# Key/value units between gate/up units, and deeper tiles for the attention's probabilities, in a decoder trunk on one core

## The chip, the core and the metric

One Trainium2 chip, one of its cores. The metric is device time in microseconds (us) of one execution. The engines are named as in the profile: PE (TensorE, matmuls), PEld (its weight loads), DVE (VectorE), ACT (ScalarE), POOL (GpSimd) and SP (SyncE, which here only issues transfers). Work tiles live in SBUF; matmuls write to PSUM, which the kernel uses in tiles of 128 x 512 fp32 (called banks below).

## What is computed

Two layers over 256 tokens of width 1024 in fp32. Each layer is half a feed-forward, a mixer, and half a feed-forward again, each behind an RMS norm and added to h:

```python
def _swiglu(x, w_gate_up, w_down):
    a, b = jnp.split(x @ w_gate_up, 2, axis=-1)      # 2 x 2816 columns
    return (jax.nn.silu(a) * b) @ w_down

for layer in range(DEPTH):
    h = h + 0.5 * _swiglu(_rmsnorm(h, ...), ...)
    hn = _rmsnorm(h, mix_norm[layer])
    if layer < N_A_LAYERS: h = h + _short_conv(hn, ...)
    else:                  h = h + _nsa(hn, ..., *shared)
    h = h + 0.5 * _swiglu(_rmsnorm(h, ...), ...)
    if layer == N_A_LAYERS - 1:
        shared = _shared_kv(h, ...)
```

So there are four feed-forwards. `_shared_kv` makes, from the h behind the second of them, the keys and values that the attention `_nsa` of the second layer uses: two slots are compressed (blocks of 32 tokens through a two-layer network), two slots of keys are normed, two slots of values are kept. Its result is needed only by the attention, that is behind the third feed-forward, which starts from the same h.

## The kernel before

**Arithmetic.** Each fp32 weight is split into two parts, `whi` (ACT casts it to the PE's fp32r format) and `wlo` (DVE subtracts: raw - whi); activations are split likewise (`hg` for normed inputs, `gg` for gated products). A product of two split numbers needs three matmuls, or a 512-column one and a 256-column one.

**Units.** The program is a list of units (`unit`, `run_units`). A unit with weights loads one `raw` tile of up to 128 x 2048 fp32 (1 MB; three buffers), splits it in two halves into `whi` and `wlo` (three buffers each), does its matmuls, and has a `post` that reads the result from PSUM. `run_units` loads three units ahead and splits two ahead.

- A *gate/up unit* (`gate_up(ft)`, 22 of them, here g0, g1, ...) does 16 pairs of matmuls into a pair of PSUM banks `pa`; its post sums the two halves and scales them on ACT and DVE (`t`), takes silu on ACT (`s`), and multiplies on POOL (`g<-s,t`). One unit later `g` is split into `gg`. 16 *down units* follow, which read `gg`.
- `shared_kv` has ten units: raw slots r0, r1 (48 matmuls of 256 columns; DVE then writes the tile `rt` out of `pa` in eight pieces, POOL adds positions to give two `rf`, ACT and DVE split them to `r`); token-major units t00, t01 (keys, both into one pair of banks) and t10, t11 (values); and compression units c00, c01, c10, c11, with only 16 matmuls of 256 columns each on 1 MB of weights. Small steps between them (`k_transposes`, `hidden`, `second_k`, `second_k2`, `second_v`) hang on a unit at a given step, by the table `KVSEQ`.

`pa` has two pairs of banks (`psA`, 2 buffers of 2 banks), used in turn by whatever unit comes next.

**Order.** The order is not the program's. A planner (`Plan.schedule`) takes every instruction with its dependencies and an estimated cost, and lays out a fixed order for each engine by list scheduling; each engine then works its own queue strictly in that order. Program order sets where two instructions stand if nothing else does, which buffer is reused after which, and which units can be split ahead of which.

**Stages.** Feed-forward 0 (from 0 us), convolution (from about 195 us), feed-forward 1 (from 295), the ten key/value units (470 to 521), feed-forward 2 (to 705), attention with its query and output projections (to 815), feed-forward 3. The calls, from the end of `program`:

```python
    u = shared_kv("n3", G_KV)
    norm_hooks("n3", u)
    ffn(2, "n3", G_FFN + 16, "n4", [G_MIX + 8], own_pool("g2"))
    u = nsa("n4", G_MIX + 8, "n5", [G_FFN + 24])
```

**Memory.** SBUF pools of the stages follow one another: `stage_pool` opens a pool `after` the one before, and the first writer of the new pool waits for all users of the old. The key/value units' tiles are in `kvp`, feed-forward 2's `gg` in `g2`, the attention's tiles in `nsap`.

**Attention.** For each of 24 steps PE computes scores (`S<-kth,qs`), DVE takes the maximum (`mx`), ACT the exponentials (`P`, five buffers), POOL weights them (`P<-P,pw`), PE transposes them (`pb<-cst,P`), ACT casts the transposes (`ph`), DVE subtracts (`pl`; `ph` and `pl` have `PB` = 2 buffers each), and PE multiplies with the values (`pc<-ph,vhl`). The output projection's first units run between these steps.

Of the kernel before, what the change touches and what calls it, by code (L numbers as in the profile page):

```python
# [134 lines left out]
class PlanPool:  # L135
    def __init__(self, plan, name, bufs, psum=False, after=None):
        self.plan, self.name, self.bufs, self.psum, self.after = plan, name, bufs, psum, after
        self.tags = {}
        self.tiles = []
        self.real = self.stack = None  # L140
# [70 lines left out]
class Plan:  # L211
# [8 lines left out]
    def pool(self, name, bufs, psum=False, after=None):  # L220
        p = PlanPool(self, name, bufs, psum, after)
        self.pools.append(p)
        return p
# [171 lines left out]
    def replay(self, tc, order, engines, stack):  # L395
        opened = {}

        def real_pool(p):
            if p.real is None:
                if p.after is not None and p.after.stack is not None:  # L400
                    p.after.stack.close()
                p.stack = ExitStack()
                kw = {"space": PSUM} if p.psum else {}
                p.real = p.stack.enter_context(tc.tile_pool(name=p.name, bufs=p.bufs, **kw))
            return p.real

        for p in self.pools:
            if p.after is None:
                real_pool(p)
# [22 lines left out]
def program(plan, a, out, ones):  # L432
# [9 lines left out]
    chain = {"sb": None, "ps": psA}  # L442

    def stage_pool(name):
        p = chain["sb"] = plan.pool(name, 1, after=chain["sb"])
        return p

    def wide_psum(name, bufs):
        wide["pool"] = chain["ps"] = plan.pool(name, bufs, psum=True, after=chain["ps"])
# [211 lines left out]
    def ffn(lf, nkey, gname, okey, ogains, pool_open):  # L661
# [6 lines left out]
        def gate_up(ft):  # L668
# [38 lines left out]
        def down(dt, c):  # L707
            def mm(wh, wl):
                if c == 0:
                    st["pd"] = psB.tile([128, 512], F32, name="pb")  # L710
                yield from halves_mm(st["pd"], (wh[:, :HALF * 128], wl[:, :HALF * 128]), c * HALF,
                                      st["gg"], c == 0, c == 1)
# [6 lines left out]
        u0 = gate_up(0)  # L719
        for ft in range(1, NF):  # L720
# [6 lines left out]
    def own_pool(name):  # L727
        def op(st):
            st["pool"] = stage_pool(name)
        return op  # L730

# [85 lines left out]
    def shared_kv(nkey, gname):  # L817
        st = {}

        def rawslot(s):  # L820
            def mm(wh, wl):
                if s == 0:
                    own_pool("kvp")(st)
                    st["kvc"] = st["pool"].tile([128, NKVC], F32, name="kvc")
                    sp.dma_start(st["kvc"], a["kvc"])
                    st["rt"] = [st["pool"].tile([128, 528], F32, name=f"rt{x}") for x in range(2)]
                    for x in range(2):
                        gp.memset(st["rt"][x][:, 512:], 0.0)
                    ac.copy(kcs, zero[:, :1].to_broadcast([128, 608]))
                    for q in range(2):  # L830
                        for ab in range(2):
                            xp = slice(64 - ab * 64, 128 - ab * 64)
                            o = kth[q][ab][xp].rearrange("p b j n -> p (b j n)")
                            ac.copy(o, zero[xp, :1].to_broadcast([64, 512]))
                st["ps"] = two_banks()
# [5 lines left out]
            def post():  # L841
                ps = st["ps"]
                R = NORM[nkey].R
                for j in range(2):
                    for gg in range(2):
                        hp = slice(gg * 64, gg * 64 + 64)
                        g = 2 * j + gg
                        for p in range(2):
                            tt(ve, st["rt"][s][p * 64:p * 64 + 64, g * 128:(g + 1) * 128],
                               ps[hp, j, p:T:2], R[hp, p:T:2], ALU.mult)  # L850
                for hh in range(2):
# [3 lines left out]
                       st["rt"][s].rearrange("p (a b) -> p a b", b=8),  # L855
# [176 lines left out]
        u0 = None  # L1032
        for name, *hooks in KVSEQ:
            u = make[name]() if name else u + 1
            u0 = u if u0 is None else u0
            for x, f in hooks:
                at_mid(u, x, side[f])
                late[u] = x
        return u0


    def nsa(nkey, gname, okey, ogains):
# [527 lines left out]
```

## Time and profile before

| | |
|---|---|
| median of three runs | 1002.56 us (999.06 to 1004.71) |
| the profiled execution's own time | 1002.02 us |
| its span | 1000.2 us |
| mean granted PE clock | 0.998 |
| PE busy | 985.0 us (98%), 5792 instructions |
| PEld busy | 859.4 us (86%) |
| DVE busy | 727.5 us (73%) |
| ACT busy | 585.7 us (59%) |
| POOL busy | 207.9 us (21%) |
| read from HBM | 175.80 MB, 177 GB/s over the span |

The profile is one execution, and lines of it give an engine, an operation, the tile it writes and those it reads (`wlo<-raw,whi`), all at line 419, since one helper issues everything; so one goes by tiles. The span runs from the first instruction to the last; the execution's own time is 1.8 us longer. Matmuls are pipelined and their ends are modelled, so PE's busy time holds short waits too. In the timeline a row is a run of like instructions, with its start, its length and, in brackets, how long the engine stood idle before it and what ended that.

### The profile page before, as it was taken

The page shows a single profiled execution, that of the slowest core. Times are in us where ns is not written, and L with a number is a line of the kernel's source. Part 1 is how long each engine was busy: PE and PEld are TensorE (multiplying, and loading weights), DVE is VectorE, ACT ScalarE, POOL GpSimd, SP SyncE. Part 2 cuts the span into 40 slices and gives each one's busy share as a digit, 9 for nine tenths or more (in the row PEclk, how much of TensorE's full clock was granted, in tenths as well). Part 3 has the DMA queues.
Part 4 walks back from the last instruction along what each step waited for, and adds up shares of the span by engine and source line. Part 5 has one row for each costly group of instructions (what it writes and reads, how often), then busy time and mean ns, then how long its engine had stood idle before and what let it go on. Part 6 is the DMA issues. An engine that isn't in the chain of part 4 may idle for free.

```text
span 1000.2 us, 15237 instructions
## 1 busy us (share of the span) xinstructions
PE 985.0 (98%) x5792; PEld 859.4 (86%) x5792; DVE 727.5 (73%) x1086; ACT 585.7 (59%) x1049; POOL 207.9 (21%) x266
## 2 busy tenths in 40 slices
PE   8999999999999999999999999999998999999998
PEld 6888888888888888889878888888897888888887
DVE  6876766688797676677889776666788787676554
ACT  8665554445465555555586656545599765555441
POOL 2211111021221111111331111100578531111100
PEclk9999999999999999999999999999999999999999
DMA  8655455655655555456366655365511245554353
GB/s 280 239 206 176 163 173 175 201 183 190 213 179 200 192 187 168 152 200 247 131 234 214 222 173 194 120 202 195 204 62 43 79 172 175 197 179 161 127 194 108
DMA packets 31033, 177.83 MB, mean 178 GB/s; under 512 B 3440, under 2 KB 6000, under 8 KB 16112
## 3 DMA queue, kind: packets, MB, share of 16 engines
q1 hardware_dynamic: 30960, 176.86, 51.4%
q8 instruction: 45, 0.74, 0.3%
q14 instruction: 28, 0.23, 0.1%
HBM read 175.80 MB, written 1.05 MB: 177 GB/s over the span
## 4 chain that ended last, share of the span: by engine, by line
PE 88%; DVE 4%; ACT 4%; issue 1%; POOL 1%; DMA 1%; SPq 0%; ACTq 0%; DVEq 0%; POOLq 0%
PE pa L419 52%; PE pb L419 29%; PE S L419 4%; PE pc L419 3%; DVE wlo L419 1%; ACT P L419 1%; ACT whi L419 1%; DVE hg L419 1%; DMA raw<-in_wgu_dram 1%; DVE px L419 0%; POOL rf L419 0%; DMA px<-in_px_dram 0%; ACT kth L419 0%; DVE s L419 0%; POOL hg L419 0%
## 5 line engine op out<-in xcount | busy, mean ns | idle before, releaser
L419 PE MATMUL pa<-hg,whi 128*128 128x512 f32 (+1 forms) x1568 | 538.8, 390 | 1.7 <-DVE hg L419 1.6
L419 DVE TENSOR_TENSOR wlo<-raw,whi 128x1024 fp32r<-128x1024 f32 (+4 forms) x383 | 412.1, 1093 | 163.8 <-ACT whi L419 162.3
L419 ACT CAST whi<-raw 128x1024 fp32r<-128x1024 f32 (+3 forms) x388 | 350.7, 927 | 198.8 <-issue 81.9
L419 PE MATMUL pa<-hg,wlo 128*128 128x256 f32 x1536 | 430.8, 281 | 0.4 <-DVE wlo L419 0.4
L419 PEld LDWEIGHTS pa<-hg,whi 128*128 128x128 f32 x1568 | 291.6, 187 | 67.8 <-DVE hg L419 3.6
L419 PEld LDWEIGHTS pa<-hg,wlo 128*128 128x128 f32 x1536 | 290.3, 189 | 1.3 <-DVE wlo L419 1.1
L419 PE MATMUL pb<-gg,whi 128*128 128x512 f32 x704 | 245.1, 394 | 0.0
L419 PE MATMUL pb<-gg,wlo 128*128 128x256 f32 x704 | 195.7, 279 | 0.0
L419 PEld LDWEIGHTS pb<-gg,whi 128*128 128x128 f32 x704 | 131.8, 187 | 30.3
L419 POOL TENSOR_TENSOR g<-s,t 128x256 f32<-128x256 f32 x88 | 71.0, 807 | 413.6 <-ACT s L419 409.7
L419 PEld LDWEIGHTS pb<-gg,wlo 128*128 128x128 f32 x704 | 132.7, 188 | 0.3
L419 ACT ACTIVATE s<-t 128x256 f32<-128x256 f32 x88 | 36.7, 417 | 137.5 <-DVE t L419 137.5
L419 POOL TENSOR_TENSOR acc<-acc,sq 128x256 f32<-128x256 f32 x36 | 33.6, 934 | 177.0 <-ACT sq L419 176.4
L419 DVE TENSOR_TENSOR t<-pa,t 128x512 f32<-128x512 f32 x94 | 64.3, 684 | 3.6 <-ACT t L419 3.5
L419 DVE TENSOR_TENSOR t<-t,R 128x512 f32<-128x512 f32 x96 | 65.7, 685 | 0.1
L419 ACT COPY t<-pa 128x512 f32<-128x512 f32 x94 | 54.2, 576 | 2.9 <-PE pa L419 2.8
L419 PE MATMUL S<-hg,whi 128*128 128x256 f32 (+1 forms) x224 | 48.7, 302 | 1.6 <-DVE hg L419 1.3
L419 DVE SCALAR_TENSOR_TENSOR px<-pb,px 128x256 f32<-128x256 f32 x56 | 23.7, 423 | 34.8 <-PE pb L419 33.9
L419 PE MATMUL pb<-hg,whi 128*128 128x512 f32 (+1 forms) x144 | 48.2, 386 | 0.0
L419 DVE TENSOR_TENSOR gg<-g,gg 128x256 fp32r<-128x256 f32 x88 | 36.8, 419 | 13.1 <-ACT gg L419 13.1
L419 ACT CAST gg<-g 128x256 fp32r<-128x256 f32 x88 | 35.4, 403 | 13.9 <-POOL g L419 12.6
L419 DVE SCALAR_TENSOR_TENSOR hg<-px,hg 128x256 fp32r<-128x256 f32 x56 | 40.1, 734 | 1.4 <-ACT hg L419 1.1
(176 smaller groups left out, 876.4 us busy)
## 6 DMA issues: line engine op xcount, KB each, us to landing
raw<-in_wgu_dram SPq DMA_DIRECT2D x86, 1024.0 KB, 4.8
raw<-in_wdn_dram SPq DMA_DIRECT2D x64, 704.0 KB, 4.2
raw<-in_wci_dram SPq DMA_DIRECT2D x8, 1024.0 KB, 5.1
raw<-in_wci_dram SPq DMA_DIRECT2D x8, 512.0 KB, 3.6
raw<-in_wco_dram SPq DMA_DIRECT2D x4, 1024.0 KB, 4.8
raw<-in_wkt_dram SPq DMA_DIRECT2D x4, 1024.0 KB, 4.8
raw<-in_wc_dram SPq DMA_DIRECT2D x4, 1024.0 KB, 4.8
raw<-in_wq_dram SPq DMA_DIRECT2D x4, 1024.0 KB, 4.8
```

The source lines that it names most:

```text
L419: getattr(engines[op.eng], op.name)(*[real(x) for x in op.args], **{k: real(v) for k, v in op.kw.items()})
```

## The change

It does five things.

1. The ten key/value units, which stood ahead of the third feed-forward, stand between its first eight gate/up units. `KVSEQ` (a list) becomes `KVAT` (which units come ahead of which gate/up unit), `shared_kv` returns a function `between(ft)`, and `ffn` calls it ahead of each `gate_up(ft)`. The order of weights is now r0 g0 r1 g1 t00 t01 g2 c00 g3 c01 g4 t10 t11 g5 c10 g6 c11 g7 g8 and so on.
2. `gg` becomes two tiles of eleven units each, in all four feed-forwards. In the third, the first half is in a pool `g20` on the right side of SBUF, which lives beside `kvp`; the second half's pool `g21` follows `kvp` (`beside_kv`). A pool may now follow several others.
3. The two `rt` tiles are allocated one by one, each in its own raw slot unit.
4. The probabilities `P` get six buffers in place of five, `ph` and `pl` four each in place of two (`PB`).
5. `dynamic_dma_scratch_size=64` at the start of the program: the scratch in SBUF that is set aside for transfers issued by POOL shrinks.

```diff
-PK, YP = 0, 1
-SB, PB, FB = 4, 2, 0
-KVSEQ = [("r0",), ("r1",), ("t00",), ("t01",), ("c00",), ("c01", (4, "k0"), (7, "k1")), ("t10", (4, "h0")),
-         ("c10", (3, "sk"), (7, "sl")), ("t11",), ("c11",), ("", (3, "h1"), (9, "sv"))]
+YP = 1
+SB, PB, FB = 4, 4, 0
+KVAT = {0: [("r0",)], 1: [("r1",)], 2: [("t00",), ("t01",)], 3: [("c00",)], 4: [("c01", (4, "k0"), (7, "k1"))],
+        5: [("t10", (4, "h0")), ("t11",)], 6: [("c10", (3, "sk"), (7, "sl"))], 7: [("c11",), ("", (3, "h1"), (9, "sv"))]}
...
-                if t.pool.after is not None:
-                    for y in t.pool.after.tiles:
+                for p in t.pool.after:
+                    for y in p.tiles:
                         op.deps.update(y.users)
...
             def fin_():
-                if ft == 0:
-                    pool_open(st)
-                    st["gg"] = st["pool"].tile([128, NF, 2, T], F32R, name="gg")
-                split(st["gg"][:, ft, 0], st["gg"][:, ft, 1], st.pop(("g", ft)))
+                if ft % HALF == 0:
+                    st["gg", ft // HALF] = pool_open(st, ft // HALF).tile([128, HALF, 2, T], F32R, name=f"gg{ft // HALF}")
+                g = st["gg", ft // HALF][:, ft % HALF]
+                split(g[:, 0], g[:, 1], st.pop(("g", ft)))
...
-        u0 = gate_up(0)
-        for ft in range(1, NF):
+        u0 = len(units)
+        for ft in range(NF):
+            if between is not None:
+                between(ft)
             gate_up(ft)
...
+    def beside_kv(st, part):
+        p = plan.pool(f"g2{part}", 1, after=[chain["kv"]] if part else chain["g1"], side=None if part else "right")
+        chain["sb"] = [p] + (chain["sb"] if part else [])
+        return p
...
+        def between(ft):
+            for name, *hooks in KVAT.get(ft, []):
+                u = make[name]() if name else len(units)
+                for x, f in hooks:
+                    at_mid(u, x, side[f])
+                    late[u] = x
+        return between
...
-                P[i, hh // 2] = st["pool"].tile([128, 2, 4, 128], F32, name="P", bufs=5)
+                P[i, hh // 2] = st["pool"].tile([128, 2, 4, 128], F32, name="P", bufs=6)
...
-    u = shared_kv("n3", G_KV)
-    pooled.update(u + i for i in range(16) if PK >> i & 1)
+    u = ffn(2, "n3", G_FFN + 16, "n4", [G_MIX + 8], beside_kv, shared_kv("n3", G_KV))
     norm_hooks("n3", u)
-    ffn(2, "n3", G_FFN + 16, "n4", [G_MIX + 8], own_pool("g2"))
...
-    nc = _bacc.Bacc("TRN2", target_bir_lowering=False, num_devices=1)
+    nc = _bacc.Bacc("TRN2", target_bir_lowering=False, num_devices=1, dynamic_dma_scratch_size=64)
```

What the planner made of it stands in the engines' queues. On SP, from the last down unit of feed-forward 1 on (`wkr`: raw slots, `wkt`: token-major, `wc`: compression, `wgu`: gate/up), before:

```order
L419 DMA raw<-in_wkr_dram 128x2048 x2
L419 DMA raw<-in_wkt_dram 128x2048 x2
L419 DMA kvc<-in_kvc_dram 128x416
L419 DMA raw<-in_wc_dram 128x2048 x2
L419 DMA raw<-in_wkt_dram 128x2048
L419 DMA raw<-in_wc_dram 128x2048
L419 DMA raw<-in_wkt_dram 128x2048
L419 DMA raw<-in_wc_dram 128x2048
L419 DMA raw<-in_wgu_dram 128x2048 x22
```

and now:

```order
L420 DMA raw<-in_wkr_dram 128x2048
L420 DMA raw<-in_wgu_dram 128x2048
L420 DMA raw<-in_wkr_dram 128x2048
L420 DMA raw<-in_wgu_dram 128x2048
L420 DMA kvc<-in_kvc_dram 128x416
L420 DMA raw<-in_wkt_dram 128x2048 x2
L420 DMA raw<-in_wgu_dram 128x2048
L420 DMA raw<-in_wc_dram 128x2048
L420 DMA raw<-in_wgu_dram 128x2048
L420 DMA raw<-in_wc_dram 128x2048
L420 DMA raw<-in_wgu_dram 128x2048
L420 DMA raw<-in_wkt_dram 128x2048 x2
```

Each compression load has a gate/up load on both sides, where four of them stood among two token-major ones.

On DVE, from the norm's statistic of this stage on (`nm`), before:

```order
L419 TENSOR_SCALAR nm<-pc 128x2
L419 TENSOR_TENSOR rt_4506<-pa,R 64x128 x8
L419 TENSOR_TENSOR wlo<-raw,whi 128x1024 x2
L419 TENSOR_TENSOR r_4654<-rf_4637,r_4654 128x8x64
L419 TENSOR_TENSOR rt_4510<-pa,R 64x128 x8
L419 TENSOR_TENSOR wlo<-raw,whi 128x1024 x2
```

and now:

```order
L420 TENSOR_SCALAR nm<-pc 128x2
L420 TENSOR_TENSOR rt<-pa,R 64x128 x8
L420 TENSOR_TENSOR wlo<-raw,whi 128x1024 x2
L420 TENSOR_TENSOR r_4640<-rf_4626,r_4640 128x8x64
L420 TENSOR_TENSOR t_4647<-pa,t_4647 128x512
L420 TENSOR_TENSOR t_4647<-t_4647,R 128x512
L420 TENSOR_TENSOR wlo<-raw,whi 128x1024 x2
L420 TENSOR_TENSOR r_4683<-rf_4636,r_4683 128x8x64
L420 TENSOR_TENSOR rt<-pa,R 64x128 x8
L420 TENSOR_TENSOR wlo<-raw,whi 128x1024 x2
L420 TENSOR_TENSOR gg_4711<-g_4699,gg_4711 128x256
```

Between the eight pieces of r0's `rt` and those of r1's there now stand two sums of g0, two more halves of a split and one more `r`; the splits are those of other units (the first pair after `rt` was t01's and is g1's; r0, g0 and r1 are split ahead of this place).

In the attention the deeper tiles reach ACT's queue. The first casts `ph` before:

```order
L419 ACTIVATE P,psum__6992<-S,nb,sc_6817 128x128 x5
L419 ACTIVATE P,psum__7176<-S,nb,sc_6817 128x256 x2
L419 CAST ph<-pb 128x512
L419 ACTIVATE P,psum__7176<-S,nb,sc_6817 128x256 x2
L419 CAST ph<-pb 128x512
L419 ACTIVATE P,psum__7176<-S,nb,sc_6817 128x256
```

and now:

```order
L420 ACTIVATE P,psum__6999<-S,nb,sc_6824 128x128 x3
L420 ACTIVATE P,psum__7176<-S,nb,sc_6824 128x256 x2
L420 CAST ph<-pb 128x512 x2
L420 ACTIVATE P,psum__7176<-S,nb,sc_6824 128x256 x2
L420 CAST whi<-raw 128x1024
L420 CAST qs_7254<-S 64x256
```

The first two casts now follow one another, with no exponentials between them, and a weight cast of the output projection has moved up. From there to the end of the attention the order differs in many places on PE, DVE, ACT and POOL; in all other stages it is the same as before.

## Rows read from the trace of the kernel before

**Rows 1.** The page: PE's line of part 1, and the chain by engine (part 4)

```profile
PE 985.0 (98%) x5792; PEld 859.4 (86%) x5792; DVE 727.5 (73%) x1086; ACT 585.7 (59%) x1049; POOL 207.9 (21%) x266
...
PE 88%; DVE 4%; ACT 4%; issue 1%; POOL 1%; DMA 1%; SPq 0%; ACTq 0%; DVEq 0%; POOLq 0%
```

**Rows 2.** Windows: length, busy PE, PEld, DVE, ACT, POOL, PE clock, DMA share, GB/s

```profile
470.50:493.60 23.10, 23.10 (x153) 21.20 (x152) 18.49 (x30) 11.31 (x17) 7.72 (x6) 1.00 0.42 148
493.60:521.10 27.50, 23.00 (x128) 18.29 (x127) 24.92 (x34) 24.82 (x41) 8.26 (x4) 1.00 0.56 200
521.10:536.30 15.20, 15.20 (x92) 13.24 (x91) 13.92 (x34) 11.97 (x23) 1.40 (x1) 1.00 0.71 261
```

**Rows 3.** Timeline of PE, key/value stage: start, length, what, [idle before <- releaser]

```profile
482.68 0.40 PE L419 MATMUL pa<-whi,hg 128*128 128x512 f32 x1
482.92 0.40 PE L419 MATMUL pa<-wlo,hg 128*128 128x512 f32 x1
...
497.61 0.39 PE L419 MATMUL pc<-wlo,r 128*128 128x256 f32 x1 [1.83 <-DVE wlo L419]
...
500.42 0.50 PE L419 MATMUL pa<-whi,hg 128*128 128x512 f32 x1 [0.58 <-ACT whi L419]
501.79 0.50 PE L419 MATMUL pa<-wlo,hg 128*128 128x512 f32 x1 [0.86 <-DVE wlo L419]
...
504.42 0.66 PE L419 MATMUL pb<-cst,kk 128*128 128x128 f32 x4 [0.49 <-POOL kk L419]
...
514.32 0.49 PE L419 MATMUL pa<-whi,hg 128*128 128x512 f32 x1 [0.28 <-ACT whi L419]
515.26 0.38 PE L419 MATMUL pc<-whi,r 128*128 128x256 f32 x1 [0.45 <-ACT whi L419]
```

**Rows 4.** Timeline of DVE, one gate/up unit of feed-forward 1

```profile
338.58 1.23 DVE L419 TENSOR_TENSOR wlo<-raw,whi 128x1024 fp32r<-128x1024 f32 x1 [1.65 <-ACT whi L419]
339.72 0.68 DVE L419 TENSOR_TENSOR t<-pa,t 128x512 f32<-128x512 f32 x1
340.32 1.22 DVE L419 TENSOR_TENSOR wlo<-raw,whi 128x1024 fp32r<-128x1024 f32 x1
...
344.12 1.23 DVE L419 TENSOR_TENSOR wlo<-raw,whi 128x1024 fp32r<-128x1024 f32 x1 [1.65 <-ACT whi L419]
```

**Rows 5.** Timeline of POOL, the same unit

```profile
342.73 0.74 POOL L419 TENSOR_TENSOR g<-s,t 128x256 f32<-128x256 f32 x1 [4.81 <-ACT s L419]
```

**Rows 6.** Timeline of DVE, start of the key/value stage

```profile
476.94 0.16 DVE L419 TENSOR_SCALAR nm<-pc 128x2 f32<-128x2 f32 x1 [1.71 <-PE pc L419]
479.12 2.41 DVE L419 TENSOR_TENSOR rt<-pa,R 64x128 f32<-64x128 f32 x8 [2.02 <-ACT R L419]
481.56 3.50 DVE L419 TENSOR_TENSOR wlo<-raw,whi 128x1024 fp32r<-128x1024 f32 x2
485.25 1.94 DVE L419 TENSOR_TENSOR r<-rf,r 128x512 fp32r<-128x512 f32 x1 [0.20 <-ACT r L419]
...
493.08 2.29 DVE L419 TENSOR_TENSOR r<-rf,r 128x512 fp32r<-128x512 f32 x2
```

**Rows 7.** Timeline of POOL, the same place

```profile
481.66 4.59 POOL L419 TENSOR_TENSOR rf<-rt,kvc 128x528 f32<-128x528 f32 x2 [3.77 <-issue]
```

**Rows 8.** The page, parts 3 and 6: the queue of the data, and a compression unit's load

```profile
q1 hardware_dynamic: 30960, 176.86, 51.4%
...
raw<-in_wc_dram SPq DMA_DIRECT2D x4, 1024.0 KB, 4.8
```

**Rows 9.** Windows of the attention, columns as in rows 2

```profile
733.00:783.00 50.00, 47.44 (x334) 40.76 (x333) 41.60 (x94) 49.31 (x155) 43.99 (x83) 0.97 0.07 23
783.00:799.00 16.00, 15.66 (x124) 14.98 (x122) 12.61 (x24) 10.04 (x16) 5.85 (x3) 1.00 0.28 90
```

**Rows 10.** Timeline of ACT, end of the attention

```profile
787.58 0.59 ACT L419 CAST ph<-pb 128x512 fp32r<-128x512 f32 x1 [0.47 <-PE pb L419]
788.48 0.59 ACT L419 CAST ph<-pb 128x512 fp32r<-128x512 f32 x1 [0.32 <-PE pb L419]
```

More of the change, by code (lines that the diff above doesn't have):

```diff
@@ L135, with __init__ @@
 class PlanPool:
-    def __init__(self, plan, name, bufs, psum=False, after=None):
-        self.plan, self.name, self.bufs, self.psum, self.after = plan, name, bufs, psum, after
+    def __init__(self, plan, name, bufs, psum=False, after=(), side=None):
+        self.plan, self.name, self.bufs, self.psum, self.after, self.side = plan, name, bufs, psum, after, side
         self.tags = {}
@@ L218, in __init__, with pool @@
         self.loader = None
-    def pool(self, name, bufs, psum=False, after=None):
-        p = PlanPool(self, name, bufs, psum, after)
+    def pool(self, name, bufs, psum=False, after=(), side=None):
+        p = PlanPool(self, name, bufs, psum, after, side)
         self.pools.append(p)
@@ L399, in real_pool @@
             if p.real is None:
-                if p.after is not None and p.after.stack is not None:
-                    p.after.stack.close()
+                for x in p.after:
+                    if x.stack is not None:
+                        x.stack.close()
                 p.stack = ExitStack()
-                kw = {"space": PSUM} if p.psum else {}
+                kw = {"space": PSUM} if p.psum else {"side": p.side} if p.side else {}
                 p.real = p.stack.enter_context(tc.tile_pool(name=p.name, bufs=p.bufs, **kw))
@@ L407, in replay @@
         for p in self.pools:
-            if p.after is None:
+            if not p.after:
                 real_pool(p)
@@ L441, in program @@
     psA = plan.pool("psA", 2, psum=True)
-    chain = {"sb": None, "ps": psA}
+    chain = {"sb": [], "ps": psA}
     def stage_pool(name):
-        p = chain["sb"] = plan.pool(name, 1, after=chain["sb"])
+        p = plan.pool(name, 1, after=chain["sb"])
+        chain["sb"] = [p]
         return p
     def wide_psum(name, bufs):
-        wide["pool"] = chain["ps"] = plan.pool(name, bufs, psum=True, after=chain["ps"])
+        wide["pool"] = chain["ps"] = plan.pool(name, bufs, psum=True, after=[chain["ps"]])
     wide = {"pool": psA}
@@ L658, in halves_sum, with ffn @@
         tt(ve, o, x, o, ALU.add)
-    def ffn(lf, nkey, gname, okey, ogains, pool_open):
+    def ffn(lf, nkey, gname, okey, ogains, pool_open, between=None):
         st = {}
@@ L710, in mm @@
                     st["pd"] = psB.tile([128, 512], F32, name="pb")
-                yield from halves_mm(st["pd"], (wh[:, :HALF * 128], wl[:, :HALF * 128]), c * HALF,
-                                      st["gg"], c == 0, c == 1)
+                yield from halves_mm(st["pd"], (wh[:, :HALF * 128], wl[:, :HALF * 128]), 0,
+                                      st["gg", c], c == 0, c == 1)
             def post():
@@ L727, in own_pool, with op @@
     def own_pool(name):
-        def op(st):
-            st["pool"] = stage_pool(name)
-        return op
+        def op(st, part=0):
+            if part == 0:
+                st["pool"] = stage_pool(name)
+            return st["pool"]
+        return op
+    def beside_kv(st, part):
+        p = plan.pool(f"g2{part}", 1, after=[chain["kv"]] if part else chain["g1"], side=None if part else "right")
+        chain["sb"] = [p] + (chain["sb"] if part else [])
+        return p
     def conv(nkey, gname, okey, ogains):
@@ L822, in mm @@
                 if s == 0:
-                    own_pool("kvp")(st)
+                    chain["g1"] = chain["sb"]
+                    chain["kv"] = own_pool("kvp")(st)
+                    chain["sb"] = []
                     st["kvc"] = st["pool"].tile([128, NKVC], F32, name="kvc")
                     sp.dma_start(st["kvc"], a["kvc"])
-                    st["rt"] = [st["pool"].tile([128, 528], F32, name=f"rt{x}") for x in range(2)]
-                    for x in range(2):
-                        gp.memset(st["rt"][x][:, 512:], 0.0)
                     ac.copy(kcs, zero[:, :1].to_broadcast([128, 608]))
@@ L834, in mm @@
                             ac.copy(o, zero[xp, :1].to_broadcast([64, 512]))
+                st["rt", s] = st["pool"].tile([128, 528], F32, name="rt")
+                gp.memset(st["rt", s][:, 512:], 0.0)
                 st["ps"] = two_banks()
@@ L854, in post @@
                     tt(gp, f.rearrange("p (a b) -> p a b", b=8),
-                       st["rt"][s].rearrange("p (a b) -> p a b", b=8),
+                       st["rt", s].rearrange("p (a b) -> p a b", b=8),
                        pos[:, None, :].to_broadcast([128, 66, 8]), ALU.add)
@@ L1031, in shared_kv @@
                 "h1": lambda: hidden(1), "sk": second_k, "sl": second_k2, "sv": second_v}
[L1032 to L1039, printed above, removed]
+        def between(ft):
[5 more added lines that the diff above has]
+        return between
     def nsa(nkey, gname, okey, ogains):
```

2 lines of the change are left out of this document (1 added, 1 removed).

## The prediction

> **What bounds the kernel now.** I read the page first, then the stages, then the waits in the stage that the change rebuilds. The page has TensorE (PE) busy for 98% of the span, and the chain that ended last runs over PE for 88% [rows 1]: time can only be won where PE waits. The places are named as in the text ahead: r0, r1 (raw slots), t00 to t11 (token-major), c00 to c11 (compression) for the key/value units, g0, g1, ... for the gate/up units of the third feed-forward. The windows say how the key/value stage fares [rows 2]: r0, r1, t00 and t01 take 23.1 us, all busy; the other six units then need 27.5 us, of which PE is busy 23.0 us while VectorE (DVE) is busy 24.9 and ScalarE (ACT) 24.8. A compression unit brings as many weights to split as any other (1 MB) for only 16 matmuls of 256 columns, so four of them in a row starve PE.
>
> The timeline of PE has six waits there, 1.83, 0.58, 0.86, 0.49, 0.28 and 0.45 us, most of them for wlo on DVE or whi on ACT [rows 3], together 4.49 us. A row of PE lasts longer than the interval to the next: t00's first matmul is 0.40 us long and the second starts after 0.24 [rows 3]. So each wait is some 0.16 us longer than the idle time shown; six of them make **5.5 us** lost.
>
> In a feed-forward there is room. One gate/up unit passes every 5.54 us (wlo at 338.58 and again at 344.12), and DVE then idles 1.65 us of it [rows 4]. POOL's product g (0.74 us) falls into that idle stretch [rows 5].
>
> **The change, part by part.** *Interleaving.* The same units are done; only their order differs. PE's work in 470.5 to 536.3 is 65.8 us less 5.5, so 60.3, and holds about 2.5 gate/up units; five and a half more at 5.54 make 90.8 us for all 18 units. DVE's busy time there is 18.49 + 24.92 + 13.92 = 57.3 us [rows 2]. One gate/up unit needs 5.54 - 1.65 = 3.9 us of it [rows 4]; eight of them are 31.2, and about 9.8 of that (three units' splits and two units' sums) is in the 57.3 already: 78.7 us. PE is the longer, by 12.1 us, so in sum it can run without a wait. What can still stop it is the order in each queue, so I walk DVE's new order from the first point at which it is late, with the durations of the rows.
>
> PE: r0 ends where it does now, at 476.8. g0 takes 5.5 and the norm's small matmuls 0.3: 482.6. r1 (about 5.8): 488.4. g1: 494.0. Then t00 needs a pair of PSUM banks, and there are two pairs, in turn: t00's is the one that r1 gives back when DVE has done r1's rt.
>
> DVE: rt of r0 as now, 479.12 to 481.53; two wlo 3.50, to 485.06; r to 487.2 [rows 6]. New behind it are g0's two t (0.60 each, the interval from t to the next row [rows 4]): 488.4. g1's bank pair is free after the first of these, 487.8, before PE wants it at 488.4. Two wlo at 1.14: 490.7. r 1.1 (two take 2.29 [rows 6]): 491.8. rt of r1 2.41: 494.2. If g0's product on POOL also holds DVE once, 0.74 us: 494.9. A hand-over to PE is some 0.2 us, so PE restarts at 495.1 in place of 494.0: a new wait of **1.1 us** (0.4 without the hold), which was nowhere before. I take 1.1, because of the next paragraph. Behind t00 and t01 (10.9 us of PE, 482.7 to 493.6 now) DVE has a lead again, and the walk finds no later wait: each compression unit now has a gate/up unit beside it, where DVE has 1.65 us to spare.
>
> *Holds between POOL and DVE.* In the stage now, two wlo that take 1.14 each elsewhere took 3.50 us while POOL ran two rf [rows 6, 7]. One wlo and then one r begin only when an rf has ended: DVE and POOL take turns, each waiting for the other's whole instruction. The change puts eight products g of 0.74 us beside a DVE that no longer idles there: at most 5.9 us more on DVE, 84.6 in all against PE's 90.8. DVE also waits 3.7 us (1.71 + 2.02) for the norm at the start [rows 6], so 2.5 us are left.
>
> The Trainium skill, page "SBUF — State Buffer", section "Who interferes with whom", speaks against the change here: a VectorE instruction with two SBUF inputs contends with a GpSimd instruction that reads SBUF, and whoever is first holds the pair of ports for its whole instruction. The rows agree (3.50 for two splits). By that rule the new wait at t00 is 1.1 us; without it, 0.4.
>
> *Loads.* SP's queue issues the same loads in the new order, each when a raw buffer is free. One takes 4.8 us to land [rows 8]; in the walk every load goes out at least 6 us ahead of its split. ACT's casts for a unit wait until PE is done with the unit three earlier, for its whi buffer; at 5.5 us a unit beside 2.0 us for two casts this costs nothing. *Scratch, split gg, pool sides*: no instruction; POOL issues no transfer (all data go over q1 [rows 8]), so its scratch is not used. Should I be wrong in this, nothing shown prices it, and I keep it in the range's slack.
>
> *Deeper tiles.* In the attention (733 to 783) ACT is busy 49.31 of 50 us [rows 9]. More buffers cannot give ACT less to do: at best 0.7 us. From 783 to 799 PE is the busy one (15.66 of 16), and its work stays. The other way, the new order may make ACT's casts ph wait for PE's transposes, as two do now for 0.47 and 0.32 us [rows 10]: 24 casts at 0.4 are 9.5 us. Nearest to the row of 49.31 is a small gain: **0.3 us**.
>
> **Sum**, against the profiled execution's 1002.02 us: 1002.02 - 5.5 + 1.1 - 0.3 = **997.3 us**. That execution lies 0.5 us under the median of the three runs, 1002.56, which themselves span 5.6 us; I leave the forecast at 997.3.
>
> **The rivals.**
> 1. *Every hold of POOL reaches PE.* If each of the eight g lands ahead of a split or sum that PE is waiting for, all 5.9 us are given back: 1002.02 - 5.5 + 0.4 + 5.9 - 0.3 = **1002.5 us**, no change. For it: the turns that the rows show, and only 2.5 us of slack. Against it: the split of a unit is two units ahead of PE, and in the feed-forwards no g costs anything. This is what the port rule of that page of the Trainium skill would do at its worst.
> 2. *Slower: the attention's casts wait.* ACT works its queue in order. If the deeper tiles put the cast ph ahead of exponentials that could run, ACT waits at each of the 24 casts for POOL's weighting and PE's transposes; at 0.4 us each, 1002.02 - 4.4 + 9.5 = **1007.1 us**. It decides from 0.18 us per cast (4.4 / 24). For it: POOL is busy 43.99 of 50 us there, so its products are often just in time. Against it: a deeper tile takes waits away, it adds none.
> 3. *The deeper tiles do more.* PE idles for small amounts in the attention, and 49.31 of 50 need not hold in a better order. If ACT's cast and exponentials pack so that the tail from 783 on, where ACT is busy only 10.04 of 16, starts 3 us earlier: **994.3 us**. Nothing in the rows shows how.
> 4. *It does not do what it says*: the order printed ahead shows the interleaving; that the tiles change nothing is within the forecast.
>
> **How the numbers follow.** Chances: forecast 0.65, rival 1 0.20, rival 2 0.07, rival 3 0.08. What a measurement of this kernel can tell from no change is about 0.5%, so bounds at 997.5 and 1007.6. The forecast lies just at the first; its own range is 995.8 (no wait at t00, and 0.7 from the attention) to 999.5 (half of what PE waits now stays), and a little over half of it counts as faster: 0.36, with rival 3 0.44. Rival 1 and the rest of the forecast are within 0.5%: 0.49, and half of rival 2 lies there. Faster 0.45, same 0.50, slower 0.05. The range for 8 in 10 leaves out rival 2 and part of rival 3: 994.3 to 1002.5.
>
> **What would show it.** Right: PE's waits from c00 on are gone, the stage of 18 units is some 4 us shorter, one wait of about 1 us ends at rt of r1 ahead of t00's first matmul, DVE's rows of two wlo show holds where a POOL g lies beside them, the attention takes as long as before. Wrong: several waits of PE for wlo behind POOL's g (rival 1), idle time of ACT before ph (rival 2), or an attention shorter by more than 1 us (rival 3).

## The result, and the profile after

| | before | after |
|---|---|---|
| median, 19 runs each | 1001.75 us (999.06 to 1005.17) | 995.23 us (992.50 to 999.84) |
| profiled execution's own time | 1002.02 us | 996.18 us |
| its span | 1000.2 us | 994.4 us |

The ratio is 0.993 with a 95% interval of 0.992 to 0.994: 6.5 us faster, 2.1 us below the forecast of 997.3 and inside its range. In the profiled spans the difference is 5.84 us. The chain still runs over PE for 88% [rows 1], but PE's share of the span has risen to 99%. The page after, PE's line of part 1 and the chain by engine:

```profile
PE 982.2 (99%) x5792; PEld 858.4 (86%) x5792; DVE 729.1 (73%) x1086; ACT 584.5 (59%) x1049; POOL 210.1 (21%) x266
...
PE 88%; ACT 5%; DVE 4%; issue 1%; POOL 1%; DMA 1%; SPq 1%; DVEq 0%; ACTq 0%
```

To see where the time went, I cut both traces at first matmuls that name a stage: of r0, of the third feed-forward's down units (`pb<-gg`), of the attention (`S<-hg`), and the last matmul into an `S` tile.

| stretch | before | after | difference |
|---|---|---|---|
| **A**: r0 to the first down unit (10 key/value, 22 gate/up units) | 173.96 | 168.80 | -5.16 |
| **D**: the 16 down units | 61.03 | 61.71 | +0.68 |
| **B**: first to last `S` (projections and attention) | 104.71 | 103.38 | -1.33 |
| all that lies outside | 660.54 | 660.51 | -0.03 |

The -0.03 outside is a balance by chance: the down units of the first feed-forward took 61.91 us before and 60.90 after, those of the second 60.90 and 61.92, with the same matmuls (last section).

Stretch A first. The windows after, columns as in [rows 2]; the first ends at PE's one wait, the second holds it:

```profile
470.50:494.03 23.53, 23.53 (x168) 21.82 (x166) 18.93 (x29) 13.00 (x19) 6.74 (x6) 1.00 0.47 159
494.03:516.10 22.07, 21.02 (x111) 18.14 (x112) 20.38 (x24) 15.02 (x21) 9.29 (x6) 1.00 0.55 200
516.10:561.30 45.20, 45.20 (x263) 39.30 (x262) 39.76 (x60) 36.02 (x68) 8.77 (x7) 1.00 0.66 230
```

PE is busy all of 90.8 us but 1.05. The six waits of [rows 3] are gone, and the new one stands where the walk put it. The timeline of PE after, ahead of t00:

```profile
493.52 0.40 PE L420 MATMUL pa<-hg,whi 128*128 128x512 f32 x1
493.75 0.28 PE L420 MATMUL pa<-hg,wlo 128*128 128x256 f32 x1
495.08 0.47 PE L420 MATMUL pa<-whi,hg 128*128 128x512 f32 x1 [1.05 <-DVE rt L420]
495.39 0.39 PE L420 MATMUL pa<-wlo,hg 128*128 128x512 f32 x1
```

The timeline of DVE after, over the walk's stretch (it answers to [rows 6]), and behind it that of POOL:

```profile
479.15 2.40 DVE L420 TENSOR_TENSOR rt<-pa,R 64x128 f32<-64x128 f32 x8 [2.26 <-ACT R L420]
481.59 3.52 DVE L420 TENSOR_TENSOR wlo<-raw,whi 128x1024 fp32r<-128x1024 f32 x2
485.30 1.94 DVE L420 TENSOR_TENSOR r<-rf,r 128x512 fp32r<-128x512 f32 x1 [0.20 <-ACT r L420]
487.27 0.69 DVE L420 TENSOR_TENSOR t<-pa,t 128x512 f32<-128x512 f32 x1
487.99 0.69 DVE L420 TENSOR_TENSOR t<-t,R 128x512 f32<-128x512 f32 x1
488.61 2.89 DVE L420 TENSOR_TENSOR wlo<-raw,whi 128x1024 fp32r<-128x1024 f32 x2
491.42 1.21 DVE L420 TENSOR_TENSOR r<-rf,r 128x512 fp32r<-128x512 f32 x1
492.54 2.39 DVE L420 TENSOR_TENSOR rt<-pa,R 64x128 f32<-64x128 f32 x8
```

```profile
481.69 4.60 POOL L420 TENSOR_TENSOR rf<-rt,kvc 128x528 f32<-128x528 f32 x2 [4.01 <-issue]
...
489.22 1.20 POOL L420 TENSOR_TENSOR g<-s,t 128x256 f32<-128x256 f32 x1 [2.75 <-ACT s L420]
```

`rt` of r1 ends at 494.93 (the walk: 494.9) and PE restarts at 495.08 (the walk: 495.1). Two `wlo` beside g0's product took 2.89 us where two without a neighbour take 2.36 (in the same trace at 507.15), and the product itself took 1.20 in place of 0.74 [rows 5]: each waited for the other.

In B the granted clock of TensorE differs too; its mean in [rows 9] is 0.97. Before, PE waited 1.47 us for a `pb` bank, until 772.01, and from 773.80 on it ran 3.41 us at the lower of its two levels (1.2 in place of 2.4 GHz). That window (columns as in [rows 2]), and PE's timeline there:

```profile
773.80:777.21 3.41, 3.41 (x12) 2.81 (x12) 1.63 (x6) 3.41 (x15) 3.33 (x7) 0.50 0.01 2
```

```profile
772.01 1.22 PE L419 MATMUL pb<-cst,P 128*128 128x128 f32 x8 [1.47 <-DVE pl L419]
...
775.47 0.63 PE L419 MATMUL pc<-ph,vhl 128*128 128x512 f32 x1
775.89 0.63 PE L419 MATMUL pc<-pl,vhl 128*128 128x512 f32 x1
```

The same matmuls after:

```profile
769.90 0.39 PE L420 MATMUL pc<-pl,vhl 128*128 128x512 f32 x1
770.13 0.40 PE L420 MATMUL pc<-ph,vhl 128*128 128x512 f32 x1
```

The next one starts after 0.42 us before and after 0.23 now; in the trace after, the clock is 1.00 throughout. So up to some 1.7 us of B before (an estimate, half of 3.41) are the clock's, more than the 1.33 by which B fell. The one profile before isn't alone in it: of the 53 runs of the kernel before that were timed beside the experiments, 38 have a mean granted clock of 0.996 to 0.998 (their mean time is 1002.5 us; 1001.6 in the other 15). None of the changed kernel's 19 runs is below 0.999. What makes the clock fall isn't shown: in *interleaving only*, below, PE waits 1.5 us in the attention as well, and the clock stays at 1.00.

### The profile page after: what moved, and what is told of

It is laid out like the page before. It is cut to its first block, busy times and chain, and to the rows that moved or that the text cites. A ratio compares the mean times of both kernels' runs of the same rounds, so it can differ in the third digit from the quotient of the medians.

```text
span 994.4 us, 15238 instructions
## 1 busy us (share of the span) xinstructions
PE 982.2 (99%) x5792; PEld 858.4 (86%) x5792; DVE 729.1 (73%) x1086; ACT 584.5 (59%) x1049; POOL 210.1 (21%) x266
## 3 DMA queue, kind: packets, MB, share of 16 engines
HBM read 175.80 MB, written 1.05 MB: 178 GB/s over the span
## 4 chain that ended last, share of the span: by engine, by line
PE 88%; ACT 5%; DVE 4%; issue 1%; POOL 1%; DMA 1%; SPq 1%; DVEq 0%; ACTq 0%
PE pa L420 53%; PE pb L420 29%; PE S L420 3%; PE pc L420 2%; ACT P L420 2%; DVE wlo L420 1%; ACT whi L420 1%; ACT ph L420 1%; DVE hg L420 1%; DMA px<-in_px_dram 1%; SPq L420 1%; DVE px L420 1%; POOL hg L420 0%; DVE s L420 0%; ACT hg L420 0%
```

## The experiments

All twelve kernels were timed beside the kernel before, with 4 to 12 runs each; ratios are to the kernel before, with 95% intervals. A, D and B are read from each kernel's own profile.

| kernel | A | B | time | ratio |
|---|---|---|---|---|
| interleaving only | 168.76 | 105.28 | 997.62 | 0.9958 (0.9943 to 0.9972) |
| deeper tiles only | 173.96 | 102.56 | 1001.16 | 0.9988 (0.9973 to 1.0004) |
| spare banks for g1 | 167.55 | 103.27 | 995.44 | 0.9931 (0.9913 to 0.9949) |
| four units first | 168.06 | 103.27 | 994.35 | 0.9930 (0.9911 to 0.9949) |
| `rf` on DVE | 167.51 | 103.29 | 993.30 | 0.9917 (0.9903 to 0.9931) |
| compression in pairs | 171.64 | 103.25 | 1000.22 | 0.9986 (0.9973 to 1.0000) |
| PB 4, P 5 | 168.68 | 104.90 | 998.18 | 0.9963 (0.9949 to 0.9977) |
| PB 2, P 6 | 168.78 | 102.42 | 993.30 | 0.9920 (0.9907 to 0.9934) |
| `rf` on DVE, PB 2, P 6 | 167.54 | 102.42 | 992.20 | 0.9896 (0.9883 to 0.9908) |
| `rf` on DVE, PB 2, P 8 | 167.55 | 104.41 | 997.12 | 0.9944 (0.9930 to 0.9957) |
| interleaving undone | 176.19 | 102.57 | 1001.04 | 0.9985 (0.9970 to 1.0000) |
| pairs, late keys | 169.07 | 103.31 | 995.84 | 0.9932 (0.9920 to 0.9944) |

### Which part of the change gives what

*Interleaving only* is the changed kernel with the attention's old tiles:

```diff
-SB, PB, FB = 4, 4, 0
+SB, PB, FB = 4, 2, 0
...
-                P[i, hh // 2] = st["pool"].tile([128, 2, 4, 128], F32, name="P", bufs=6)
+                P[i, hh // 2] = st["pool"].tile([128, 2, 4, 128], F32, name="P", bufs=5)
```

> The changed kernel with the old tiles: P five buffers, ph and pl two each; the interleaving and the smaller scratch stay. Measure: A = time from r0's first matmul to the first down unit of the third feed-forward (174.0 us before, 168.8 changed), B = from the first to the last matmul into S, the attention with its projections (104.7 before, 103.4 changed). Theory (the interleaving gives 5.2 us, the tiles 1.3): A 168.8, B 104.7, about 996.5 us on the scale where before has 1001.75. Rival (the tiles give most and the stage is only shifted): A about 173, time near 1000.

*Deeper tiles only* edits the kernel before:

```diff
-SB, PB, FB = 4, 2, 0
+SB, PB, FB = 4, 4, 0
...
-                P[i, hh // 2] = st["pool"].tile([128, 2, 4, 128], F32, name="P", bufs=5)
+                P[i, hh // 2] = st["pool"].tile([128, 2, 4, 128], F32, name="P", bufs=6)
...
-    nc = _bacc.Bacc("TRN2", target_bir_lowering=False, num_devices=1)
+    nc = _bacc.Bacc("TRN2", target_bir_lowering=False, num_devices=1, dynamic_dma_scratch_size=64)
```

> The kernel before with P six buffers, ph and pl four each, and the smaller scratch; the key/value units stand ahead of the feed-forward as before. Theory: A 174.0, B 103.4, about 1000.4 us. Rival 1 (ACT bounds the attention, so tiles can't matter and the 1.3 us of the one profile are its scatter): B 104.7, 1001.7 us. Rival 2 (they give most): B below 102, time below 999.

*Interleaving undone* is the changed kernel with all ten units ahead of g0 again, in their old order:

```diff
+KVAT = {0: [("r0",), ("r1",), ("t00",), ("t01",), ("c00",), ("c01", (4, "k0"), (7, "k1")), ("t10", (4, "h0")),
+            ("c10", (3, "sk"), (7, "sl")), ("t11",), ("c11",), ("", (3, "h1"), (9, "sv"))]}
```

> The changed kernel with only the interleaving undone: all ten key/value units ahead of the first gate/up unit in the order of the kernel before; gg stays split in two tiles, on the sides of SBUF that the change chose, the tiles of the attention stay deeper, the scratch stays small. Theory (the stage's gain is the order alone): 173.96 us from r0 to the first down unit and about 1001 in time, as the kernel with the deeper tiles only. Rival (the split or the place of gg matters for the stage): 169 to 173 us. For the down units of the third feed-forward, 60.91 us in both kernels without interleaving and 61.59 in all with it: 61.59 if that hangs on the place of gg, 60.91 if it hangs on the order.

Interleaving alone keeps the whole of A (168.76) and is 0.4% faster; deeper tiles alone leave A as before, and their time can't be told from the kernel before. Both missed in B: 105.28 for 104.7 (and 997.62 us for 996.5) with interleaving only, 102.56 for 103.4 with the deeper tiles only. So the interleaving reaches B as well: with it, the planner orders the attention otherwise. *Interleaving undone* and *deeper tiles only* share one order there, and B is 102.57 and 102.56; the same tiles in the changed kernel take 103.38.

With only the order undone, PE's waits of before are back one for one. Its waits in 470 to 580 (releaser; total, times, longest):

```profile
PE pc L420 <- DVE wlo L420: 1.8, 1, 1.8
PE pa L420 <- DVE wlo L420: 0.9, 1, 0.9
PE pa L420 <- ACT whi L420: 0.9, 2, 0.6
PE pb L420 <- POOL kk L420: 0.5, 1, 0.5
PE pc L420 <- ACT whi L420: 0.4, 1, 0.4
```

So the order is the cause of A's gain, and neither the split nor the place of `gg` is. That A reads 176.19 and not 173.96 there, outside both expectations, is something else: its gate/up units ran at the slower of two paces (228 matmuls from 590 to 630 us, where before has 233), told in the last section. Its down units took 61.50 us from first to last matmul; in all eleven interleaved kernels they took 61.57 to 61.59, in the two kernels with the old `gg` 60.91. So in these profiles D's 0.7 us go with the change's `gg`, not with the order. But only two of them have the old `gg`, and the down units of the other feed-forwards took 60.9, 61.0 or 61.9 us from execution to execution (last section). What the change's `gg` costs in other executions isn't shown.

### The new wait at t00, and the hold of POOL

*Spare banks* gives g1 two single banks of another pool, so that t00 need not wait for r1's pair:

```diff
-            return (nkey, ft) in (("n0", 2), ("n5", 0))
+            return (nkey, ft) in (("n0", 2), ("n3", 1), ("n5", 0))
```

> The changed kernel; the second gate/up unit of the third feed-forward (g1) uses two of the single banks pb in place of a pair pa, so that t00 gets the pair that g0 gives back and needn't wait for r1's rt. Theory (the one wait left in the stage, 1.05 us ahead of t00's first matmul, hangs on the pair of banks alone): no wait of PE between r0 and g8 above 0.3 us, A 167.8, about 1 us faster than the change, 994.2. Rival (DVE is late, the banks only show it): PE waits as long a little later, for t01's wlo or g2's pair, A 168.8.

*Four units first* has r0 r1 t00 t01 ahead of g0 and one gate/up unit between the compression units as before:

```diff
+KVAT = {0: [("r0",), ("r1",), ("t00",), ("t01",)], 1: [("c00",)], 2: [("c01", (4, "k0"), (7, "k1"))],
+        3: [("t10", (4, "h0")), ("t11",)], 4: [("c10", (3, "sk"), (7, "sl"))], 5: [("c11",), ("", (3, "h1"), (9, "sv"))]}
```

> The changed kernel; r0, r1, t00, t01 stand together ahead of g0 as before the change, and only the other six key/value units stand among gate/up units: g0 c00 g1 c01 g2 t10 t11 g3 c10 g4 c11 g5. Theory (all that PE lost was at the compression units, where a gate/up unit beside each of them is enough, and the new wait at t00 is gone because its pair hangs on r0's rt): A 167.8 to 168.0, 994.2 us. Rival (DVE needs the slack of two more gate/up units): waits for wlo return, at c01 to c11, A 169 to 172.

*`rf` on DVE* moves the four additions behind `rt`, and nothing else:

```diff
-                    tt(gp, f.rearrange("p (a b) -> p a b", b=8),
+                    tt(ve, f.rearrange("p (a b) -> p a b", b=8),
```

> The changed kernel with the four additions rf (128x528) on VectorE in place of GpSimd; nothing else is edited, the planner lays out the order anew. Theory (GpSimd's rf and g hold VectorE's splits): the two wlo behind rt of r0, 3.52 us in the changed kernel, take 2.3 (two at 1.14), the four rf cost VectorE some 0.7 each, and the rt of r1 ends near 491.6 on the changed kernel's clock in place of 494.9, so PE's wait of 1.05 us ahead of t00 is gone: from r0's first matmul to the first down unit 167.7 us in place of 168.8. Rival (the splits are long there for another reason, and VectorE only gets 2.8 us more to do): they stay at 3.5 us, the wait ahead of t00 stays at 1 us or grows, and the stage takes 168.8 us or more.

In none of the three is the wait for `rt` left, and A falls to 168.06, 167.55 and 167.51. The wait hung on the bank pair. In the times the gain of 0.1% can be told from the changed kernel in none of the three by itself: the intervals overlap.

`rf` on DVE also settles the hold. The timeline of DVE in that kernel, same place:

```profile
479.23 2.40 DVE L420 TENSOR_TENSOR rt<-pa,R 64x128 f32<-64x128 f32 x8 [2.26 <-ACT R L420]
481.66 1.23 DVE L420 TENSOR_TENSOR wlo<-raw,whi 128x1024 fp32r<-128x1024 f32 x1
482.81 1.32 DVE L420 TENSOR_TENSOR rf<-rt,kvc 128x528 f32<-128x528 f32 x2
484.04 1.22 DVE L420 TENSOR_TENSOR wlo<-raw,whi 128x1024 fp32r<-128x1024 f32 x1
485.29 0.69 DVE L420 TENSOR_TENSOR t<-pa,t 128x512 f32<-128x512 f32 x1
485.90 2.35 DVE L420 TENSOR_TENSOR wlo<-raw,whi 128x1024 fp32r<-128x1024 f32 x2
488.17 1.19 DVE L420 TENSOR_TENSOR r<-rf,r 128x512 fp32r<-128x512 f32 x1
489.28 2.39 DVE L420 TENSOR_TENSOR rt<-pa,R 64x128 f32<-64x128 f32 x8
```

The same two splits take 2.45 us, not 3.52. DVE does the two `rf` itself and is through with all four at 485.26; in the changed kernel the splits alone kept it until 485.11. Two additions that took POOL 4.60 us cost DVE 1.32. `rt` of r1 ends at 491.67, 3.3 us earlier, and PE waits nowhere in the stage. Only part of the 3.3 is holds: behind these splits DVE is no earlier. In the new order one `r` (1.94 us in the changed kernel, and 0.20 idle ahead of it) and one `t` (0.69) stand behind `rt` in place of ahead of it, and no product holds the next splits (0.54).

### Why the order helps: one gate/up unit for each compression unit?

*Compression in pairs*:

```diff
+KVAT = {0: [("r0",)], 1: [("r1",)], 2: [("t00",), ("t01",)], 3: [("c00",), ("c01", (4, "k0"), (7, "k1"))], 4: [("t10", (4, "h0")), ("t11",)],
+        5: [("c10", (3, "sk"), (7, "sl")), ("c11",), ("", (3, "h1"), (9, "sv"))]}
```

> The changed kernel with the compression units in pairs: c00 and c01 follow one another ahead of the fourth gate/up unit, t10 and t11 ahead of the fifth, c10 and c11 ahead of the sixth. Theory (what starves PE is two weights to split in a row with little PE work each; a gate/up unit beside each one is what helps): waits for wlo or whi come back at c01 and c11, 0.6 to 1.8 us each as before, and the stage takes 170.5 to 172 us in place of 168.8, a time of 997 to 998. Rival (it is enough that some gate/up units stand in the stage, since splits run two units ahead and VectorE has 12 us to spare in sum): no wait over 0.3 us besides the one at t00, 168.8 to 169.3 us, a time as the changed kernel's, about 995.

A was 171.64 us, inside what my theory said, but for another reason. The time, 1000.22, is above the 997 to 998 that it said: 7 of the 12 runs have a mean granted clock of 0.997 or 0.998, and average 1001.2 us, the other five 998.1. PE waits for no split. It waits 1.89 us ahead of the second transpose of the keys. The timelines of PE, DVE and POOL there:

```profile
518.61 0.66 PE L420 MATMUL pb<-cst,kk 128*128 128x128 f32 x4 [1.89 <-DVE kk L420]
```

```profile
514.19 1.01 DVE L420 TENSOR_SCALAR s<-s 128x8 f32<-128x8 f32 x1
515.12 1.21 DVE L420 TENSOR_TENSOR wlo<-raw,whi 128x1024 fp32r<-128x1024 f32 x1
516.26 0.68 DVE L420 TENSOR_TENSOR t<-pa,t 128x512 f32<-128x512 f32 x1
517.86 0.69 DVE L420 TENSOR_TENSOR kk<-kk,r 128x512 f32<-128x512 f32 x1 [0.93 <-POOL r L420]
```

```profile
511.36 2.69 POOL L420 TENSOR_TENSOR r<-s,neghalf 128x8 f32<-128x8 f32 x1 [4.05 <-ACT whi L420]
514.13 1.05 POOL L420 TENSOR_TENSOR kk<-kk,r 128x512 f32<-128x512 f32 x1
515.28 2.54 POOL L420 TENSOR_TENSOR r<-s,neghalf 128x8 f32<-128x8 f32 x1
```

The keys' norm is a chain of its own: two `r` of 2.5 to 2.7 us each on POOL, and `kk` on DVE behind the second. The transposes hang on c01, and with no gate/up unit between c00 and c01 they come before that chain is through. *Pairs, late keys* moves them to the gate/up unit behind (a part of `KVAT`, against the kernel with the pairs):

```diff
-3: [("c00",), ("c01", (4, "k0"), (7, "k1"))],
+3: [("c00",), ("c01",), ("", (4, "k0"), (7, "k1"))],
```

> The kernel with the compression units in pairs, with the transposes of the keys (k0, k1) moved from c01 to the gate/up unit behind it. There PE waited 1.89 us for kk of the second token-major unit, ahead of those transposes, and for no split. Theory (the stage needs gate/up units ahead of the transposes, so that the norm of the keys is done, not one beside each compression unit): the wait is gone, the stage takes 168.8 to 169.3 us in place of 171.64, and the time is that of the changed kernel, 995. Rival (pairs starve PE of splits, which the wait for kk hid by giving VectorE time): waits for wlo or whi of 1 us or more come up at c01, c11 or behind, and the stage stays above 170.5 us.

The wait is gone, A is 169.07 and the time 995.84, as with the change; the largest wait for a split is 0.15 us. So one gate/up unit beside each compression unit is not needed. Pairs in this order cost 0.3 us of A; what starved PE was four of them with no gate/up unit in 27 us.

### Which tile pays in the attention

*PB 4, P 5* undoes the sixth P in the changed kernel, *PB 2, P 6* the deeper `ph` and `pl`:

```diff
-                P[i, hh // 2] = st["pool"].tile([128, 2, 4, 128], F32, name="P", bufs=6)
+                P[i, hh // 2] = st["pool"].tile([128, 2, 4, 128], F32, name="P", bufs=5)
```

> The changed kernel with five buffers for P as before, ph and pl keep four. The attention (first to last score matmul) took 103.38 us in the changed kernel and 105.28 with neither. Theory (the deeper ph and pl do it: the casts no longer wait for the matmuls with the values): 103.2 to 103.7 us, and 995 in time. Rival (the sixth P does it): 105 us, and 997.

```diff
-SB, PB, FB = 4, 4, 0
+SB, PB, FB = 4, 2, 0
```

> The changed kernel with two buffers each for ph and pl as before, P keeps six. Theory (ph and pl do it): the attention takes 105 us from first to last score matmul, and 997 in time. Rival (the sixth P does it): 103.2 to 103.7 us, and 995.

My theory was that `ph` and `pl` pay; the rival was right, and by more than its 103.2 to 103.7. The sixth P alone makes B 102.42 us, 2.86 less than with neither (105.28); four `ph` and `pl` alone give 0.38, and added to the sixth P they cost 1.0 (103.38). PE's waits in the attention, first with neither (interleaving only), then with the sixth P alone:

```profile
PE pb L420 <- DVE pl L420: 2.8, 4, 1.5
...
PE pc L420 <- ACT ph L420: 0.5, 2, 0.3
```

```profile
PE pb L420 <- DVE pl L420: 0.8, 2, 0.4
```

The wait for `pl` is that of PE's transposes for a `pb` bank that `pl` gives back; it falls from 2.8 to 0.8 us and no wait for `ph` is left. In the changed kernel three waits of score matmuls for an `S` bank, which the exponentials that write P give back, have come up in their place:

```profile
PE S L420 <- ACT P L420: 1.0, 3, 0.5
PE pb L420 <- DVE pl L420: 1.0, 3, 0.4
```

Each depth also gives the attention a new order, so these differences hold depth and order together. Without the interleaving, six P with four `ph` and `pl` reach 102.56, so that the deeper `ph` and `pl` cost 1.0 is shown for the interleaved orders alone.

*`rf` on DVE, PB 2, P 6* puts the edit of `rf` and the last one together, and *P 8* also uses the room that the smaller PB leaves:

```diff
-                P[i, hh // 2] = st["pool"].tile([128, 2, 4, 128], F32, name="P", bufs=6)
+                P[i, hh // 2] = st["pool"].tile([128, 2, 4, 128], F32, name="P", bufs=8)
```

> The changed kernel with rf on VectorE and with two buffers each for ph and pl (P keeps six). Each alone took 1.3 us from the key/value stage (167.51 in place of 168.80) and 1.0 us from the attention (102.42 in place of 103.38). Theory (they lie in different stages and add up): stage 167.5, attention 102.4, a time of about 993, 2 us under the changed kernel. Rival (the planner lays out the attention anew and the gain there was luck of its order): attention 103.3 or more.

> As the kernel with rf on VectorE and two buffers for ph and pl, with eight buffers for P in place of six, in the room that ph and pl leave. Theory (the score work can run further ahead of the casts): attention 101.5 to 102.4 us. Rival (six are enough, what is left in the attention is the work of ScalarE and TensorE): 102.4 to 103.3 us, no change in time.

The two gains add up: A 167.54 and B 102.42. At 992.20 us, ratio 0.9896 (0.9883 to 0.9908), its interval lies below the changed kernel's (0.992 to 0.994), so in its four runs it beats both kernels. Not all of that is A and B: outside of A, D and B its profile has 658.4 us, the changed kernel's 660.5, mainly because none of its feed-forwards goes at the slower pace of the last section. Nor is the rival settled, since the order of the attention is the same as in *PB 2, P 6*. Eight P were neither better nor the same but 2.0 us worse in B. The planner's order differs in many places with each depth; why this one is worse was not looked into.

## Why the prediction was right, and where it was off

- **The interleaving, -5.5.** Right in place and mechanism, too small. The kernels without a wait in the stage have A = 167.5, so before it lost 173.96 - 167.51 = 6.45 us. I priced a wait at its idle time plus 0.16. The new wait of 1.05 cost 168.80 - 167.51 = 1.29: 0.16 in the last interval, and 0.08 because the second matmul behind it starts after 0.31 us rather than 0.23 (rows of PE above). Six waits at 0.24 make 4.49 + 1.44 = 5.9. Some of the last 0.5 is in stalls too short to show as idle time: at 504.83 and 508.20 the next matmul starts after 0.32 and 0.31 us, where 0.23 is usual; the rest I can't place. And the interleaving wasn't confined to its stage: it gave the attention another order, which I had not reckoned with.
- **The new wait at t00, +1.1.** Idle time 1.05, same releaser, same instant; all told it cost 1.29. The hold that I had taken into it was there: 2.89 for the two splits, 0.53 over two without a neighbour (I took 0.74). That the walk met 494.9 is partly luck: its other rows came 0.2 us late in sum. The rule of the Trainium skill that I set beside the rows ("SBUF — State Buffer", section "Who interferes with whom") agrees with `rf` on DVE: 3.52 us became 2.45 when GpSimd no longer ran beside them.
- **Rival 1, every hold reaches PE.** It did not: with eight products of POOL in the stage, PE had one wait. DVE had the room that the sum gave it.
- **"Scratch, split gg, pool sides: no instruction".** This step failed: I put the change of `gg` at nothing, and D grew by 0.68 us without one instruction more; with the change's `gg` it was 61.5 us or more from first to last matmul in all twelve profiles, while two have 60.91 with the old one. I also argued only over whether the scratch is used, not over its room: the first half of `gg` in `g20` takes 22 KB of each partition beside `kvp` (11 x 2 x 256 fp32). No run has the interleaving with the default scratch, so whether it needs the smaller one isn't shown. Point 3 of the change is more than it says as well: both `rt` have one name in a pool of one buffer, so r1's takes r0's place once r0's `rf` have read it. They had by 486.29, and `rt` of r1 started at 492.54, so it cost nothing.
- **Deeper tiles, -0.3.** Too small: B fell by 1.33, and by my own sign (more than 1 us) rival 3 has its part. But the 1.33 is no price of the tiles. It holds the fall of the clock in the trace before (up to 1.7 us) and the other order that the interleaving gives the attention. Beside the interleaving, with the clock at 1.00 in both traces, the tiles give 105.28 - 103.38 = 1.90; without it 104.71 - 102.56 = 2.15, the fall of the clock included. I argued from ACT's 49.31 of 50 busy us [rows 9] that no more than 0.7 could be had. But the stretch needn't hold the same work: in the corresponding 50 us after, PE does more of it, 349 matmuls in place of 334, while ACT is again almost full. PE's wait of 1.47 us at 772.01 for a `pb` bank and the clock of 0.97 in [rows 9] were what to price: both stood in the trace before. The window after, columns as in [rows 9]:

```profile
728.00:778.00 50.00, 47.56 (x349) 41.54 (x349) 41.07 (x96) 48.77 (x157) 42.76 (x82) 1.00 0.01 2
```

- **Rival 2, casts ph wait.** It did not come: ACT is busy 48.77 of 50 us after, and no wait of PE for `ph` is left.
- **The sum.** By what was measured: 1002.02 - 6.45 + 1.29 + 0.68 - 1.33 = 996.2, the profiled execution's 996.18. Forecast and sum differ by 1.1 us, and that they do by no more is partly luck: I had 0.95 too little for the interleaving and 1.03 for B, against 0.87 too little for the new wait and D. The rest of the way to the median of 995.23 is the scatter of executions.

## What to carry to other kernels

A stage in which PE starves because its units bring many bytes for few matmuls is mended by spreading those units among others that have vector time to spare; the walk through the vector engine's new order says where the next wait will be, and a bank pair that an earlier unit holds is the first place to look. An engine that is full says little about what a deeper buffer is worth: price the waits of the engine that sets the end, read the granted clock in the same row, and try each depth by itself, since one tile paid here and the other took part of it back. Where a planner lays out each kernel anew, compare the orders before a difference is put down to a buffer. Small vector additions on POOL can cost DVE nearly as much by their holds (1.07 us here) as doing them would (1.32).

## What was not expected of the hardware

**Two paces of TensorE at one clock.** A gate/up unit takes 5.547 us of PE in some feed-forwards and 5.654 in others, with no wait, the same instructions and a granted clock of 1.00. The windows of 40 us count it, first of the kernel before (second and fourth feed-forward), then of *`rf` on DVE, PB 2, P 6* (fourth):

```profile
360.00:400.00 40.00, 40.00 (x232) 35.28 (x232) 27.95 (x36) 23.61 (x38) 5.27 (x8) 1.00 0.52 179
...
880.00:920.00 40.00, 40.00 (x228) 34.68 (x227) 27.70 (x36) 22.84 (x37) 5.16 (x7) 1.00 0.52 180
```

```profile
880.00:920.00 40.00, 40.00 (x233) 35.24 (x232) 27.23 (x38) 22.73 (x37) 5.92 (x8) 1.00 0.51 170
```

228 matmuls in one case, 232 or 233 in the other. Of the 56 feed-forwards in the fourteen profiles, 20 took the slower pace, each for all the gate/up units measured (its last eight). The first feed-forward, which the kernels with the change share, had either pace, so the stage's own instructions don't set it. One feed-forward at the slower pace costs 22 x 0.107 = 2.35 us, and four can. That is enough for most of the 6 us between the fastest and the slowest run of one kernel, though only the profiled executions show it. The profiles of before and after have the slower pace in the fourth feed-forward both, so the comparison of their spans holds as far as this goes. What sets it stays open.

**The down units have it too.** Their 22 matmuls take 3.70 or about 3.77 us from first to last. In the first, second and fourth feed-forward of the fourteen profiles all 16 units together took 60.9 us in 15 cases, 61.0 to 61.1 in 19 (those with the slower pace ahead of them) and 61.9 in 8, and one kernel can have more than one of these. In D of the changed kernel both occur in turn, and the pattern repeats after six units: 3.70, 3.72, 3.76, 3.76, 3.70, 3.77. Six is three weight buffers times two halves of `gg`, so the pace may hang on where a weight buffer and a half of `gg` lie; that was only argued, no kernel moved them alone.
